# A router softmax on one core: hand-written synchronisation around all but the first loads, one filler matmul a trip, two rows cast early

## The chip, the cores and the metric

The kernel runs on one core of one Trainium2 chip. The metric is the device time of one execution in microseconds, the median of three runs. The profile is of one execution; its span runs from the first to the last profiled instruction and is a little shorter than the measured time.

## The reference

```python
# x: 16 x 512 x 1024 fp32, router_weights: 1024 x 8 fp32
logits = np.matmul(x, router_weights)
exp_logits = np.exp(logits - np.max(logits, axis=-1, keepdims=True))
return (exp_logits / np.sum(exp_logits, axis=-1, keepdims=True)).astype(np.float32)
```

There are 8192 tokens. Each has 1024 features, which are reduced to 8 logits, and a softmax runs over the 8. Nearly all of the traffic is the read of `x`, 33.6 MB.

## The kernel before

A token is named by a partition `p` (of P = 128) and a "row" `j` (of J = 64): row j is one tile of 128 tokens by 1024 features. Every row takes the same way. It is loaded and cast to bf16 in `x_all`; TensorE (PE) turns it in eight transposes of 128 x 128 (`loop_turn`, `turn`), five into the PSUM tile `ptv` and three into `pts`; VectorE copies the five to `xTv` and ScalarE the three to `xTs`; PE multiplies the eight chunks with the weights (`multiply`, eight matmuls with 8 columns each) into one place of the PSUM tile `lg`. After a group of eight rows VectorE and ScalarE do its softmax in five steps (`group` on VectorE, `power` on ScalarE), which are strewn between the copies.

All five engines are programmed by hand, with a semaphore for each dependence, inside one block of the framework, `tc.tile_critical()` (line 65), to which the framework adds an entry and an exit with a barrier of all engines (its instructions carry the lines 65 and 439 in the profile).

- **Loads.** SyncE (SP) issues rows 0 to 3 as fp32 into `x_f32`, in two transfers of two rows (line 130, semaphores `s_f`). ScalarE issues the weights (line 298) and casts the four rows to bf16 (line 304). GpSimd (POOL) issues all other rows with a cast on the way (line 150): twelve loads of four rows, three of two and five of one; row 63 comes in three pieces (line 163). Between the second and third of its loads GpSimd makes the identity and the filler's operand (lines 154 to 160).
- **Passing on.** SyncE waits for each cast and each landing and adds the number of rows to `s_xr` (lines 133 to 138), from which PE takes one for each row it turns (line 194). Later SyncE issues two stores of the result (lines 141 and 143) and waits for both (line 145).
- **The loop.** PE runs a hardware loop of 31 trips (line 263). A trip is: a filler matmul of 512 columns into a spare bank, whose result nobody reads; row 2t+1 turned; row 2t multiplied; a second filler; row 2t+2 turned; row 2t+1 multiplied. Instructions made by the helpers `again` have the line of what they were copied from, so in the loop all transposes have line 259 and all products and fillers line 246.
- **ScalarE's order.** Four casts, then one copy out of `pts` a row (line 319) and one exponential a group (line 309).
- **The tail.** After the loop the pieces of row 63 are turned, row 62 and row 63 are multiplied, and the last three rows get a softmax of their own (lines 376 to 413).

```python
        for k in range(LOADS[0]):
            if k % 2 == 0:
                act.wait_ge(s_f[k // 2], 16)
            act.copy(xa[:, k, :], x_f32[:, k, :]).then_inc(s_cast, 1)
```

Of the kernel before, what the change touches and what calls it, by code (L numbers as in the profile page):

```python
# [10 lines left out]
def kernel(  # L11
# [6 lines left out]
    nc = tc.nc  # L18
# [46 lines left out]
    with tc.tile_critical():  # L65
        X_AT = place[0]
        xa = sb("x_all", [P, J, D], bf16)
        x_f32 = sb("x_f32", [P, LOADS[0], D], fp32)
        identity = sb("identity", [P, P], bf16)
        ident = sb("ident", [P, P], fp32)  # L70
        w8 = sb("w8", [KO, P, N], fp32)
        w_bf = sb("w_bf", [P, KO, N], bf16)
        outv = sb("outv", [P, J, N], fp32)
        filler = sb("filler", [P, 512], bf16)
        xTv = [sb(f"xTv{i}", [P, VN, P], bf16) for i in range(2)]
        xTs = [sb(f"xTs{i}", [P, SN, P], bf16) for i in range(2)]
        xTz = [sb(f"xTz{i}", [P, n, P], bf16) for i, n in enumerate(PIECES)]
        mx = [sb(f"mx{i}", [P, G, 1], fp32) for i in range(2)]
        ex = [sb(f"ex{i}", [P, G, N], fp32) for i in range(2)]
        ev = [sb(f"ev{i}", [P, G, N], fp32) for i in range(2)]  # L80
        ssum = [sb(f"ssum{i}", [P, G, 1], fp32) for i in range(2)]
        inv = [sb(f"inv{i}", [P, G, 1], fp32) for i in range(2)]
        low = sb("low", [P, ALONE], fp32)
        ev3 = sb("ev3", [P, ALONE, N], fp32)
        sum3 = sb("sum3", [P, ALONE, 1], fp32)
        inv3 = sb("inv3", [P, ALONE, 1], fp32)


        LG_AT = 0x2000000
        lg = ps("lg", [P, 2, G, 64], fp32)  # L90
        ptv = [ps(f"ptv{i}", [P, 8, P], bf16) for i in range(2)]
        pts = [ps(f"pts{i}", [P, 8, P], bf16) for i in range(2)]
        spare = ps("spare", [P, 512], fp32)
        extra = ps("extra", [P, 8, 64], fp32)

        sem = tc.alloc_semaphore
        s_f = [sem(f"s_f{i}") for i in range(2)]
        s_w = sem("s_w")
        s_ld = [sem(f"s_ld{i}") for i in range(len(LOADS))]
        s_z = [sem(f"s_z{i}") for i in range(len(PIECES))]  # L100
        s_cast = sem("s_cast")
        s_m = sem("s_m")
        s_d = sem("s_d")
        s_id = sem("s_id")
        s_idb = sem("s_idb")
        s_fill = sem("s_fill")
        s_wt = sem("s_wt")
        s_wb = sem("s_wb")
        s_xr = sem("s_xr")
        s_tv = sem("s_tv")  # L110
        s_ts = sem("s_ts")
        s_cv = [sem(f"s_cv{i}") for i in range(2)]
        s_cs = [sem(f"s_cs{i}") for i in range(2)]
        s_zt = [sem(f"s_zt{i}") for i in range(len(PIECES))]
        s_zc = [sem(f"s_zc{i}") for i in range(len(PIECES))]
        s_p = sem("s_p")
        s_ex = sem("s_ex")
        s_ev = sem("s_ev")
        s_low = sem("s_low")
        s_e3 = sem("s_e3")  # L120
        s_out = sem("s_out")
        s_st = [sem(f"s_st{i}") for i in range(2)]

        first = [sum(LOADS[:i]) for i in range(len(LOADS))]
        cols = [sum(PIECES[:i]) for i in range(len(PIECES))]


        sp = nc.sync
        for i in range(2):
            sp.dma_start(  # L130
                out=x_f32[:, 2 * i:2 * i + 2, :], in_=x_rows[:, 2 * i:2 * i + 2, :]
            ).then_inc(s_f[i], 16)
        for k in range(LOADS[0]):
            sp.wait_ge(s_cast, k + 1).then_inc(s_xr, 1)
        for i in range(1, len(LOADS)):
            n = min(LOADS[i], LOOP_T + 1 - first[i])
            if n > 0:
                sp.wait_ge(s_ld[i], 16).then_inc(s_xr, n)
        sp.wait_ge(s_z[0], 16)
        sp.wait_ge(s_out, NG - 1)  # L140
        sp.dma_start(out=out_rows[:, 0:DONE, :], in_=outv[:, 0:DONE, :]).then_inc(s_st[0], 16)
        sp.wait_ge(s_out, NG + 1)
        sp.dma_start(out=out_rows[:, DONE:J, :], in_=outv[:, DONE:J, :]).then_inc(s_st[1], 16)
        for s in s_st:
            sp.wait_ge(s, 16)


        for i, r in enumerate(LOADS):
            if i:
                nc.gpsimd.dma_start(  # L150
                    out=xa[:, first[i]:first[i] + r, :], in_=x_rows[:, first[i]:first[i] + r, :]
                ).then_inc(s_ld[i], 16)
            if i == 2:
                nc.gpsimd.memset(ident, 0.0).then_inc(s_m, 1)
                nc.gpsimd.wait_ge(s_m, 1)
                nc.gpsimd.affine_select(  # L156
                    out=ident, in_=ident, compare_op=ALU.not_equal, fill=1.0, base=0,
                    pattern=[[-1, P]], channel_multiplier=1,
                ).then_inc(s_id, 1)
                nc.gpsimd.memset(filler, 0.5).then_inc(s_fill, 1)  # L160
        for i, n in enumerate(PIECES):
            c = slice(cols[i] * P, (cols[i] + n) * P)
            nc.gpsimd.dma_start(out=xa[:, J - 1, c], in_=x_rows[:, J - 1, c]).then_inc(s_z[i], 16)  # L163


        pe = nc.tensor
        r_x = [pe.alloc_register(f"rx{c}") for c in range(KO)]
        r_l = pe.alloc_register("rl")
        for c, r in enumerate(r_x):

            pe.reg_mov(r, X_AT + D * 2 + c * P * 2 + (P - 1) * 2)
        pe.reg_mov(r_l, LG_AT + 256 * SKIP)

        def at(ap, like, r):
            return mybir.RegisterAccessPattern(
                ap=ap, dtype=like.dtype, memsetref=like.tensor.name + "_set",
                regref=r.name, is_regloc_offset=False, reg_ap_offset=r.name,
                const_ap_offset=0, const_sub_tensor_id=0,
            )

        def again(like, **k):
            return pe.add_instruction(copy.replace(like, name=f"I-{nc.next_id()}", **k))

        def turn_ap(b, c):
            return (ptv if c < VN else pts)[b][:, c if c < VN else c - VN, :]

        def chunk(b, c):
            return xTv[b][:, c, :] if c < VN else xTs[b][:, c - VN, :]

        def loop_turn(b):  # L190

            for c in range(KO):
                if c == 0:
                    pe.wait_ge(s_xr, 1).then_inc(s_xr, -1)
                t = again(
                    turn_like,
                    ins=(turn_like.ins[0], at([[J * D, P], [1, P]], xa, r_x[c])),
                    outs=(pe.lower_ap(turn_ap(b, c), opt=False),),
                )
                if c == VN - 1:  # L200
                    t.then_inc(s_tv, 1)
                if c == KO - 1:
                    t.then_inc(s_ts, 1)
            for c in range(KO):
                pe.reg_add(r_x[c], r_x[c], D * 2)

        def turn(j):
            for c in range(KO):
                t = pe.transpose(turn_ap(j % 2, c), xa[:, j, c * P:(c + 1) * P], identity)
                if c == VN - 1:  # L210
                    t.then_inc(s_tv, 1)
                if c == KO - 1:
                    t.then_inc(s_ts, 1)
            return t

        def multiply(b, dst):

            for c in range(KO):
                if c == 0:
                    pe.wait_ge(s_cv[b], 1).then_inc(s_cv[b], -1)  # L220
                if c == VN:
                    pe.wait_ge(s_cs[b], 1).then_inc(s_cs[b], -1)  # L222
                if dst is None:
                    m = again(
                        mult_like,
                        ins=(
                            pe.lower_ap(w_bf[:, c, :], opt=False),
                            pe.lower_ap(chunk(b, c), opt=False, for_matmul_weights=True),
                        ),
                        outs=(at([[2 * G * 64, P], [1, N]], lg, r_l),),  # L230
                        start_tensor_calc=(c == 0),
                        stop_tensor_calc=(c == KO - 1),
                    )
                else:
                    m = pe.matmul(
                        dst, lhsT=chunk(b, c), rhs=w_bf[:, c, :],
                        start=(c == 0), stop=(c == KO - 1),
                    )
                if c == KO - 1:
                    m.then_inc(s_p, 1)  # L240
# [203 lines left out]
```

## Time and profile before

| | |
|---|---|
| time, median of 3 runs (lowest to highest) | 93.55 us (93.3 to 93.58) |
| span of the profiled execution | 91.8 us |
| PE busy on matmuls | 66.0 us, 72% |
| VectorE, ScalarE, GpSimd busy | 38.2, 38.4, 13.4 us |
| read from HBM, mean rate over the span | 33.59 MB, 369 GB/s |
| filler matmuls, count and mean | 63, 400 ns |

An entry such as `L342 DVE COPY xTv<-ptv` names the line, the engine, the operation and the tiles it writes and reads. PEld are PE's loads of the stationary operand, which run beside its matmuls. A name with a q (SPq) is the engine's queue: waits, semaphores and issues of transfers, which are not counted as busy. Matmuls overlap, so their durations do not add up; the distance between starts tells the pace. In the row of slices each digit is a fortieth of the span, 2.3 us, and 9 means nine tenths busy or more.

### The profile page before, as it was taken

How to read it: one execution, taken by the hardware profiler on the slowest of the kernel's cores; microseconds unless marked ns; L12 is line 12 of the kernel's file. 1: busy time of each engine (PE TensorE's matmuls, PEld its weight loads, DVE VectorE, ACT ScalarE, POOL GpSimd, SP SyncE). 2: the span in 40 equal slices, each digit the busy share in tenths (PEclk: the TensorE clock that was granted, in tenths of full speed). 3: DMA queues.
4: the chain of work that ended last, by engine and by line, in shares of the span. 5: the costliest groups of instructions: out<-in, count | busy, mean ns of one | idle time of the engine just before them, and what ended most of it. 6: DMA issues, size and time to landing. Idle time of an engine off the chain costs nothing.

```text
span 91.8 us, 3012 instructions
## 1 busy us (share of the span) xinstructions
PE 66.0 (72%) x1096; PEld 58.3 (63%) x1096; DVE 38.2 (42%) x113; ACT 38.4 (42%) x80; POOL 13.4 (15%) x30
## 2 busy tenths in 40 slices
PE   0519102998888888888888888888888888888300
PEld 0408001888877777888777777777777888777100
DVE  0202100245554555455445545554554455447500
ACT  3253038245444544454445444544444454447300
POOL 4899994000000000000000000000000000000000
PEclk9999999999999999999999999999999999999975
DMA  2999999999999999999999999999999999960000
GB/s 43 361 339 278 286 225 200 225 228 211 211 207 228 221 203 203 229 225 211 200 221 228 218 203 207 228 225 214 189 220 209 210 209 208 202 132 26 0 20 0
DMA packets 3906, 18.14 MB, mean 198 GB/s; under 512 B 568, under 2 KB 1080, under 8 KB 2112
## 3 DMA queue, kind: packets, MB, share of 16 engines
q0 software_dynamic: 3312, 15.73, 83.8%
q1 hardware_dynamic: 576, 2.36, 6.7%
q10 hardware_dynamic: 16, 0.03, 0.3%
q14 instruction: 2, 0.02, 0.0%
HBM read 33.59 MB, written 0.26 MB: 369 GB/s over the span
## 4 chain that ended last, share of the span: by engine, by line
PE 66%; issue 9%; DVE 1%; ACT 1%
PE spare L246 22%; PE ptv L259 19%; PE lg L246 12%; PE pts L259 12%; PE spare L290 1%; ACT xTz L329 1%; ACT xTs L319 0%; DVE low L378 0%; ACT ev L313 0%; DVE outv L369 0%; DVE inv L409 0%; DVE outv L411 0%; DVE sum L407 0%; DVE inv L365 0%
## 5 line engine op out<-in xcount | busy, mean ns | idle before, releaser
L342 DVE COPY xTv<-ptv 128x640 bf16<-128x640 bf16 x63 | 31.0, 491 | 43.5 <-PE ptv L259 40.5
L319 ACT COPY xTs<-pts 128x384 bf16<-128x384 bf16 x63 | 30.0, 478 | 37.0 <-PE pts L259 37.0
L246 PE MATMUL spare<-filler 128*128 128x512 bf16 x63 | 25.2, 400 | 7.9 <-issue 7.9
L259 PE MATMUL ptv<-identity,x_all 128*128 128x128 bf16 x311 | 28.8, 225 | 1.9 <-PEq L258 1.9
L259 PEld LDWEIGHTS ptv<-identity,x_all 128*128 (+1 forms) x311 | 23.2, 100 | 6.4 <-issue 3.4
L259 PE MATMUL pts<-identity,x_all 128*128 128x128 bf16 x186 | 21.3, 225 | 0.0
L246 PE MATMUL lg<-w_bf,xTs 128*128 128x8 bf16 x186 | 13.4, 166 | 6.1 <-PEq L222 6.1
L246 PE MATMUL lg<-w_bf,xTv 128*128 128x8 bf16 x310 | 16.9, 167 | 0.0
L246 PEld LDWEIGHTS lg<-w_bf,xTv 128*128 128x128 bf16 x310 | 14.7, 98 | 0.0
L259 PEld LDWEIGHTS pts<-identity,x_all 128*128 x186 | 13.6, 101 | 0.0
L246 PEld LDWEIGHTS lg<-w_bf,xTs 128*128 128x128 bf16 x186 | 9.1, 96 | 6.1 <-issue 6.1
L246 PEld LDWEIGHTS spare<-filler 128*128 128x128 bf16 x63 | 6.1, 97 | 10.5 <-issue 10.4
L150 POOL DMA_DIRECT2D x_all<-in_x_dram x20 | 10.7, 615 | 1.0 <-SPq L65 1.0
L304 ACT CAST x_all<-x_f 128x1024 bf16<-128x1024 f32 x4 | 4.0, 1042 | 8.2 <-DMA x_f<-in_x_dram 8.2
L253 PE MATMUL extra<-ident,w 8*128 8x8 f32 x8 | 1.0, 255 | 3.4 <-POOL ident L156 3.4
L253 PEld LDWEIGHTS extra<-ident,w 8*128 8x128 f32 x8 | 0.9, 198 | 3.4 <-POOL ident L156 3.4
L309 ACT ACTIVATE ev<-ex 128x64 f32<-128x64 f32 (+1 forms) x8 | 2.0, 254 | 0.3 <-DVE ex L354 0.3
L336 DVE CAST identity<-ident 128x128 bf16<-128x128 f32 x1 | 0.5, 518 | 3.4 <-POOL ident L156 3.4
L304 ACT ACT_TABLE_LOAD x1 | 1.3, 1283 | 1.5 <-SPq L65 1.5
L163 POOL DMA_DIRECT2D x_all<-in_x_dram x3 | 1.7, 704 | 0.0
L369 DVE TENSOR_TENSOR outv<-ev,inv 128x64 f32<-128x64 f32 (+1 forms) x8 | 1.7, 214 | 0.0
L354 DVE TENSOR_TENSOR ex<-lg,mx 128x64 f32<-128x64 f32 (+1 forms) x8 | 1.7, 213 | 0.0
(36 smaller groups left out, 14.8 us busy)
## 6 DMA issues: line engine op xcount, KB each, us to landing
x_all<-in_x_dram POOLq DMA_DIRECT2D x12, 1024.0 KB, 34.2
x_f<-in_x_dram SPq DMA_DIRECT2D x2, 1024.0 KB, 8.2
x_all<-in_x_dram POOLq DMA_DIRECT2D x3, 512.0 KB, 62.4
x_all<-in_x_dram POOLq DMA_DIRECT2D x5, 256.0 KB, 66.5
out_dram<-outv SPq DMA_DIRECT2D x1, 212.0 KB, 2.0
x_all<-in_x_dram POOLq DMA_DIRECT2D x1, 128.0 KB, 68.1
x_all<-in_x_dram POOLq DMA_DIRECT2D x2, 64.0 KB, 67.9
out_dram<-outv SPq DMA_DIRECT2D x1, 44.0 KB, 1.5
```

Source lines behind the costliest of these rows:

```text
L150: nc.gpsimd.dma_start(out=xa[:, first[i]:first[i] + r, :], in_=x_rows[:, first[i]:first[i] + r, :]).then_inc(s_ld[i], 16)
L163: nc.gpsimd.dma_start(out=xa[:, J - 1, c], in_=x_rows[:, J - 1, c]).then_inc(s_z[i], 16)
L246: return pe.matmul(spare, lhsT=filler[:, 0:P], rhs=filler, start=True, stop=True)
L253: t = pe.transpose(w_ps[:, n, :], w8[:, :, n], ident[0:KO, 0:KO])
L259: turn_like = pe.transpose(turn_ap(0, 0), xa[:, 0, 0:P], identity).ins
L290: m = pe.matmul(alone[2], lhsT=xTz[i][:, c, :], rhs=w_bf[:, cols[i] + c, :], start=(k == 0), stop=(k == KO - 1),)
L304: act.copy(xa[:, k, :], x_f32[:, k, :]).then_inc(s_cast, 1)
L309: act.activation(ev[g % 2][:, 0:n, :], ex[g % 2][:, 0:n, :], func=Exp).then_inc(s_ev, 1)
L319: act.copy(xTs[j % 2], pts[j % 2][:, 0:SN, :]).then_inc(s_cs[j % 2], 1)
L342: dve.tensor_copy(out=xTv[j % 2], in_=ptv[j % 2][:, 0:VN, :]).then_inc(s_cv[j % 2], 1)
L354: dve.tensor_tensor(out=ex[b][:, 0:n, :], in0=rows, in1=mx[b][:, 0:n, :].broadcast_to([P, n, N]), op=ALU.subtract,).then_inc(s_ex, 1)
L369: dve.tensor_tensor(out=outv[:, starts[g]:ends[g], :], in0=ev[b][:, 0:n, :], in1=inv[b][:, 0:n, :].broadcast_to([P, n, N]), op=ALU.mult,). ...
```

## The change

There are four edits.

1. The framework's part holds only the issue of the first three transfers (two of `x_f32`, the weights), in `tc.manual_schedule()`. It is closed right behind them with `tc.close()` and `tc.compile()`, which put its closing barrier and its clear of semaphores there. Everything else is written to the engines afterwards, and no instruction of the framework follows the wait for the last store. The purpose is to have no closing barrier at the end.
2. For that, the semaphores of the first transfers lie outside those that the framework clears, and are taken back by hand (`then_inc(s_f[i], -16)`, `then_inc(s_w, -16)`); GpSimd gets a drain of its own behind its loads.
3. The second filler of a trip goes: 32 filler matmuls remain of 63.
4. ScalarE casts rows 0 and 1, does the first two copies out of PSUM, and only then waits for and casts rows 2 and 3, so that it need not hold back the first rows' copies until the second load has landed.

The diff, without the lines in which only the indentation changed:

```diff
-    with tc.tile_critical():
...
-        s_f = [sem(f"s_f{i}") for i in range(2)]
-        s_w = sem("s_w")
+    s_f = [nc.alloc_semaphore(f"s_f{i}") for i in range(2)]
+    s_w = nc.alloc_semaphore("s_w")
...
-        sp = nc.sync
-        for i in range(2):
-            sp.dma_start(
+    with tc.manual_schedule():
+        early = [
+            nc.sync.dma_start(
                 out=x_f32[:, 2 * i:2 * i + 2, :], in_=x_rows[:, 2 * i:2 * i + 2, :]
             ).then_inc(s_f[i], 16)
+            for i in range(2)
+        ]
+        early.append(
+            nc.scalar.dma_start(
+                out=w8, in_=router_weights.rearrange("(ko ki) n -> ko ki n", ko=KO)
+            ).then_inc(s_w, 16)
+        )
+        for t in early:
+            tc.no_tile_sem_insts.add(t.ins.name)
+    tc.close()
+    tc.compile()
+
+    sp = nc.sync
...
         nc.gpsimd.dma_start(out=xa[:, J - 1, c], in_=x_rows[:, J - 1, c]).then_inc(s_z[i], 16)
+
+    nc.gpsimd.drain()
...
-        pe.wait_ge(s_w, 16)
+    pe.wait_ge(s_w, 16).then_inc(s_w, -16)
...
     with pe.Fori(0, TRIPS):
         fill()
         loop_turn(1)
         multiply(0, None)
-        fill()
         loop_turn(0)
         multiply(1, None)
...
-        act.dma_start(
-            out=w8, in_=router_weights.rearrange("(ko ki) n -> ko ki n", ko=KO)
-        ).then_inc(s_w, 16)
-        for k in range(LOADS[0]):
-            if k % 2 == 0:
-                act.wait_ge(s_f[k // 2], 16)
-            act.copy(xa[:, k, :], x_f32[:, k, :]).then_inc(s_cast, 1)
+    def cast(i):
+        act.wait_ge(s_f[i], 16).then_inc(s_f[i], -16)
+        for k in (2 * i, 2 * i + 1):
+            act.copy(xa[:, k, :], x_f32[:, k, :]).then_inc(s_cast, 1)
...
+    cast(0)
     for j in range(J - 2):
         act_copy(j)
+        if j == 1:
+            cast(1)
         if j - 1 in ends[:-1]:
             power(ends.index(j - 1))
```

## The prediction

> **What bounds the kernel now.** I read the page first: span 91.8 us of 93.55 us measured, so 1.75 us lie outside the profile. The sections on engine time and on slices say
>
> ```profile
> PE 66.0 (72%) x1096; PEld 58.3 (63%) x1096; DVE 38.2 (42%) x113; ACT 38.4 (42%) x80; POOL 13.4 (15%) x30
> ...
> DMA  2999999999999999999999999999999999960000
> ```
>
> PE is at eight tenths through the middle, and the transfers are at nine from slice 1 to 34 (2.3 to 80 us) and end before the program does. Two streams run side by side, and the question is which sets the end. The waits of the SyncE queue, which passes each landing on to PE, give the pace of the loads:
>
> ```profile
> SPq L138 <- DMA x_all<-in_x_dram: 65.0, 19, 5.3
> ```
>
> Taken in stretches of 5 us, nearly each wait for a load of four rows is 4.8 us, and with the instructions between the landings are 4.85 us apart: 1.21 us a row. The view of line 138 has its last instruction, which passes on row 62, the last row of the loop:
>
> ```profile
> L138 SPq EVENT_SEMAPHORE  x20: 17/17/17, 15.1 to 80.7; - x20
> ```
>
> Next the timeline of PE, one trip in the middle (start, duration):
>
> ```profile
> 50.99 0.39 PE L246 MATMUL spare<-filler 128*128 128x512 bf16 x1 [0.30 <-issue]
> 51.21 0.44 PE L259 MATMUL ptv<-identity,x_all 128*128 128x128 bf16 x5
> ...
> 51.88 0.38 PE L246 MATMUL spare<-filler 128*128 128x512 bf16 x1
> 52.10 0.44 PE L259 MATMUL ptv<-identity,x_all 128*128 128x128 bf16 x5
> ...
> 53.19 0.39 PE L246 MATMUL spare<-filler 128*128 128x512 bf16 x1 [0.30 <-issue]
> ```
>
> A trip is 2.20 us for two rows, 1.10 us a row, and PE waits for no load in it: the idle time is the loop's own 0.30 us. So PE is a little faster than the loads but late: it starts on row 1 in earnest at 15.7 us and chases. Has it caught up at the end? The tail of the timeline:
>
> ```profile
> 82.96 0.44 PE L259 MATMUL ptv<-identity,x_all 128*128 128x128 bf16 x5
> ...
> 84.84 0.27 PE L279 MATMUL ptv<-identity,x_all 128*128 128x128 bf16 x2
> ...
> 86.87 0.34 SPq L143 DMA_DIRECT2D out_dram<-outv  x1
> ```
>
> Row 62 is turned at 82.96 although it was there at 80.7: PE is still 2.3 us behind. From there to the last store's issue are 3.91 us. What follows is not work. The store's semaphore is seen at 88.4; then the framework closes (views of lines 65 and 439):
>
> ```profile
> L65 POOLq DRAIN  x1: 1934/1934/1934, 88.7 to 88.7; - x1
> ...
> L439 POOLq EVENT_SEMAPHORE_RANGE_CLEAR  x1: 374/374/374, 91.1 to 91.1; - x1
> ```
>
> A drain of GpSimd, a barrier, a clear and a barrier: 88.44 to 91.79, 3.35 us.
>
> [...] Four rows are 2.10 MB read in 4.85 us, 432 GB/s[...]. [...] The trace shows the change once: the five turns of a row take 0.74 us until 20.2 us and 0.44 after. [...]
>
> **The change, part by part.**
> (1) Closing barrier gone: no instruction stands after SyncE's wait for the last store. All 3.35 us from 88.44 on lie on the path. The drain now written by hand follows GpSimd's issues, which end at 14.9 us now: even 1.93 us of it lie beside the loop. Gain 3.35 us.
> (2) One filler a trip fewer. It holds PE from 51.88 to 52.10, 0.22 us; a trip becomes 1.98 us, 0.99 us a row. VectorE's and ScalarE's copies (0.49 and 0.48 us a row) do not bind: the copy of row 33 ends at 52.18, its product began at 52.54 and would begin at 52.32. Over 31 trips this is 6.8 us, but loads give two rows only every 2.42 us, so all PE can win is its lag. It gains (2.42 - 1.98) x 2 = 0.88 us per four rows; from a lag of about 5 us (rows 12 to 15 landed at 22.8, row 12 is turned at 28) it has caught up after six loads, near row 36. After that PE waits for loads. At the end: row 62 is passed on at 80.68; from such an event to PE's first turn took 0.15 to 0.2 us in the case of row 0 (cast done 6.73, PE 6.9). Turn at 80.87 instead of 82.96: gain 2.1 us. The 3.91 us behind it stay: turn, product of row 61, VectorE's maximum, ScalarE's two copies, last products, softmax of three rows. Its other inputs, the pieces of row 63, land by 81.3, 81.6 and 82.0 (packet records) and are needed 0.95, 1.2 and 1.9 us after the turn: 81.8, 82.1, 82.7. No wait.
> (3) The framework's part is short and closes early. Behind SyncE's two loads stands a barrier. SyncE issues perhaps 0.07 us earlier (a NOP goes), until 1.74; then drains, a clear and barriers of the kind that now take 90.67 to 91.74, 1.07 us. GpSimd then issues its first load at about 2.8 instead of 1.44. If a drain there takes 1.93 us more, it is 4.7; if the barrier overlaps the issues, 2. I take 2.8. What hides it: x_f32 alone fills the engines (410 GB/s between 4 and 5 us, before GpSimd's first packet at 5.3) and its 2.1 MB need until about 7.4. GpSimd's first packet moves to 6.7 (5.9 to 8.6), so the stream has a gap of 0 to 1.2 us; I take 0.1. Queued behind GpSimd are ident, filler and through them PE's first turns, all done by 6 us, before row 0 is cast. The two take-backs of 16 are one more semaphore instruction each (17 ns on ScalarE's queue, 51 on PE's, in the view of line 439), ahead of waits that are longer: 0.
> (4) ScalarE: rows 0 and 1 are cast, then copied out of PSUM, then rows 2 and 3. Today the first copy waits behind all four casts, until 14.9. The order of the built program also has the table load (1.28 us) behind the wait for the first load, so the first cast moves from 5.7 to about 7. PE's product of row 0 no longer waits from 9.4 to 15.5. All of this changes when PE starts, and the lag is gone by the end anyway: 0 us.
> Sum: 3.35 + 2.1 - 0.1 = 5.35, 93.55 - 5.35 = 88.2 us.
>
> **The rivals.**
> A, as summed: 88.2 us, 74 in 100.
> B, PE cools while it waits. With one filler it is busy 62% of the time: 32 turns of 56 ns, 32 products of 25 and two fillers of 215 are 3.0 us in 4.85. At the slow rate a half trip with filler takes 1.49 us (17.23 to 18.73), without about 1.11, four rows 5.2 us; that is more than 4.85, so a cold PE never waits[...]. The tail would lose about 0.3 us on each group of eight turns and some on products, 0.8 in all: 89.0 us, 13 in 100.
> C, the end of the profile isn't the end of the measurement: if the 3.35 us are replaced by a wait outside the span, 91.5. For it: 1.75 us are outside now. Against: nothing shows them to overlap the close. 5 in 100.
> D, the early barrier waits for the loads in flight: GpSimd issues at about 8.6 and its packets start at 12.5, while x_f32 ends at 7.4: 5.1 us of idle engines, 93.3 us. SyncE's drains are 7 ns, but none stands before an open transfer. 3 in 100.
> E, slower: PE stays at the slow rate for good. 31 trips of 1.49 + 1.11 = 2.60 from 15 us end at 95.6; the 3.1 us after the loop (83.8 to 86.87) and 0.8 more put the store at 99.5, its landing 1.55 later at 101.1: 102.8 us measured. For it: PE is slow from 6.9 to 20.2 today. Against: at that rate it is never idle. 5 in 100 with everything else that ends above 93.8.
>
> **How the numbers follow.** A with the early gap (0 to 1.2) and half a microsecond on the load's rate holds 87.3 to 89.4, B reaches 90; C and above are left out: 87.3 to 90.0. Faster by more than 0.3% is A, B and C with a part of D: 0.93; within it the rest of D: 0.02; slower E: 0.05.
>
> **What would show it.** Right: the span ends with the wait for the last store, about 86.4; PE's idle time before turns is put down to loads or to SyncE from about row 36; row 62 is turned within 0.3 us of its landing; store issue 3.9 us later; the first GpSimd load near 2.8 and the last landing still near 82. Wrong: turns of 0.74 us past 25 us (B, E), a first GpSimd load after 5 us (D), a span near 86 with a time above 90 (C).

## The result and the profile after

The changed kernel takes 89.04 us (median of 4 runs, 88.88 to 89.33), the kernel before 93.56 us beside it: a ratio of 0.951, 95% interval 0.944 to 0.957. It is 4.5 us faster. The forecast was 88.2 us with a range of 87.3 to 90.0.

The page of the changed kernel, engine time, granted clock and transfers by slices (each digit is a fortieth of 87.8 us):

```profile
span 87.8 us, 2937 instructions
...
PE 64.1 (73%) x1065; PEld 56.7 (65%) x1065; DVE 38.4 (44%) x113; ACT 38.4 (44%) x80; POOL 13.5 (15%) x30
...
PEclk9999999999999999999759999999958999999998
DMA  3999999999999999999999999999999999999200
```

The transfers fill the span as before. What is new stands in the row of the clock: twice, near the 20th and the 30th slice, PE was granted half speed (0.50, for 3.41 us each time). The same row of the kernel before:

```profile
PEclk9999999999999999999999999999999999999975
```

The lines of the framework and of the last wait, from the views by line:

```profile
L144 POOLq EVENT_SEMAPHORE  x4: 17/17/17, 1.9 to 2.7; - x4
...
L144 POOLq EVENT_SEMAPHORE_RANGE_CLEAR  x1: 330/330/330, 2.2 to 2.2; - x1
...
L160 SPq EVENT_SEMAPHORE  x1: 28/28/28, 87.8 to 87.8; - x1
```

The same wait in the kernel before:

```profile
L145 SPq EVENT_SEMAPHORE  x1: 17/17/17, 88.4 to 88.4; - x1
```

The barrier and the clear are over at 2.7 us, beside the first transfers, and the wait for the last store (line 160, at 87.76) is the end of the span. Before, 3.37 us followed it (88.42 to 91.79), now 0.03.

The loop, from PE's timeline (start, duration; row 57 is turned, that is transposed, at 77.16, row 58 at 77.96):

```profile
76.94 0.39 PE L263 MATMUL spare<-filler 128*128 128x512 bf16 x1 [0.35 <-issue]
77.16 0.44 PE L276 MATMUL ptv<-identity,x_all 128*128 128x128 bf16 x5
...
77.96 0.44 PE L276 MATMUL ptv<-identity,x_all 128*128 128x128 bf16 x5
...
79.10 0.39 PE L263 MATMUL spare<-filler 128*128 128x512 bf16 x1 [0.35 <-issue]
```

A trip is 2.16 us; it was 2.20. The second filler held PE for 0.22 us, and its removal shortens the trip by 0.04. The tail (row 62 turned, last piece turned, last store) and the line that passes row 62 on:

```profile
82.28 0.44 PE L276 MATMUL ptv<-identity,x_all 128*128 128x128 bf16 x5
...
84.16 0.27 PE L295 MATMUL ptv<-identity,x_all 128*128 128x128 bf16 x2
...
86.20 0.34 SPq L158 DMA_DIRECT2D out_dram<-outv  x1
```

```profile
L153 SPq EVENT_SEMAPHORE  x20: 17/17/17, 13.0 to 80.4; - x20
```

Row 62 is passed on at 80.4 and turned at 82.28, 1.9 us later. Before it was 2.3. From its turn to the last store's issue are 3.92 us, as before (3.91).

So the 4.5 us are, between the two profiled executions: 3.34 us behind the last store's wait; 0.67 us by which the tail comes earlier; and 0.46 us outside the span, which was 1.77 us in the profiled execution before and is 1.32 now.

### The profile page after: what moved, and what is told of

It reads as the page before. It is cut to its first block, busy times and chain, and to the rows that moved or that the text cites. A ratio compares the mean times of both kernels' runs of the same rounds, so it can differ in the third digit from the quotient of the medians.

```text
span 87.8 us, 2937 instructions
## 1 busy us (share of the span) xinstructions
PE 64.1 (73%) x1065; PEld 56.7 (65%) x1065; DVE 38.4 (44%) x113; ACT 38.4 (44%) x80; POOL 13.5 (15%) x30
## 3 DMA queue, kind: packets, MB, share of 16 engines
q0 software_dynamic: 3312, 15.73, 87.7%
## 5 line engine op out<-in xcount | busy, mean ns | idle before, releaser
L276 PE MATMUL ptv<-identity,x_all 128*128 128x128 bf16 x311 | 30.3, 233 | 6.2 <-PEq L211 4.8
L276 PEld LDWEIGHTS ptv<-identity,x_all 128*128 (+1 forms) x311 | 22.3, 103 | 10.4 <-issue 7.7
L276 PE MATMUL pts<-identity,x_all 128*128 128x128 bf16 x186 | 22.0, 230 | 0.0
L263 PE MATMUL spare<-filler 128*128 128x512 bf16 x32 | 13.7, 429 | 9.0 <-issue 8.9
L276 PEld LDWEIGHTS pts<-identity,x_all 128*128 x186 | 14.3, 105 | 0.0
L263 PEld LDWEIGHTS spare<-filler 128*128 128x128 bf16 x32 | 3.1, 98 | 11.6 <-issue 11.5
L318 ACT ACT_TABLE_LOAD x1 | 1.3, 1283 | 5.6 <-ACTq L316 5.6
L367 DVE TENSOR_REDUCE mx<-lg 128x8 f32<-128x64 f32 (+1 forms) x8 | 1.7, 214 | 0.0
```

The lines of the kernel that those rows point to most:

```text
L263: return pe.matmul(spare, lhsT=filler[:, 0:P], rhs=filler, start=True, stop=True)
L276: turn_like = pe.transpose(turn_ap(0, 0), xa[:, 0, 0:P], identity).ins
L367: dve.reduce_max(mx[b][:, 0:n, 0], rows, axis=X).then_inc(s_d, 1)
```

## The experiments

All are timed beside the kernel before, whose medians in these comparisons were 93.86 to 93.89 us. The changed kernel was timed beside a median of 93.56. So the ratios are what to compare, and a difference of medians between the changed kernel and another can be off by 0.3 us.

Two explanations of the lag at the end, the 1.9 us, stood against each other. The *backlog* theory: rows 48 to 51 land together, so at that moment PE has four rows before it, of which three count as late; from there to the landing of row 62 PE needs seven trips and the loads 13.6 us, and what PE needs more than that is the lag. The *clock* theory: the half-rate windows make it. On the trip there were two as well: the *array* binds it (then a filler costs its 0.22 us), or PE's own *instruction queue*, with its semaphore, register and branch instructions.

**Edits 1 and 2 alone**: the changed kernel with the second filler and the four casts as before.

```diff
         multiply(0, None)
+        fill()
         loop_turn(0)
...
     cast(0)
+    cast(1)
     for j in range(J - 2):
         act_copy(j)
-        if j == 1:
-            cast(1)
```

> Edits 1 and 2 alone: the framework's early close, with two fillers a trip and all four casts ahead of the first copies. Backlog theory: a trip stays 2.20 us and the start is earlier, so PE still meets the last four-row load with little lag; the span loses the 3.35 us behind the last store's wait and about 0.3 us at the start, the time the same and 0.4 us more that lie outside the span: 89.4 us. Rival, the gain is shared by all edits: well above that, 90.5 or more.

Measured: 89.55 us, ratio 0.958 (0.952 to 0.963). By the ratios the early close alone brings 4.2 of the changed kernel's 4.9%. The gain isn't shared by all edits. The early close also brings most of the earlier tail, with two fillers still in the trip. Row 62 in this kernel's PE timeline:

```profile
82.39 0.44 PE L276 MATMUL ptv<-identity,x_all 128*128 128x128 bf16 x5
```

That is 0.57 us earlier than the 82.96 of the kernel before, of the 0.68 that the changed kernel reaches.

**Edit 3 alone**: the kernel before without the second filler.

```diff
         multiply(0, None)
-        fill()
         loop_turn(0)
```

> Edit 3 alone: the kernel before with the second filler of a trip taken out. If the array's time binds the trip: 1.98 us, PE catches up and row 62 is turned 1.5 to 2 us earlier, 91.6 us. If PE's instruction queue binds it: trip 2.16 us, row 62 at most 0.5 us earlier, 93.1 us.

Measured: 93.13 us, ratio 0.993 (0.991 to 0.996): 0.7%, and a trip of 2.16 to 2.18 us. The array does not set the trip; that the instruction queue does is shown further down. The 0.7 and the 4.2 add up to the whole, but the sum is an accident, for at the tail the two do the same work. Here row 62 is turned at 82.09, 0.87 us earlier than before, since the shorter trips bring PE level with the loads at row 48 (it is turned 0.17 us after it lands); the early close alone has 0.57, and both together have 0.68.

**The second filler put back** into the changed kernel (the first hunk of edits 1 and 2 alone).

> The changed kernel with the second filler put back. Queue theory: trip 2.20 us instead of 2.16, over the eight trips after the last four-row load 0.3 us, time 89.3. Array theory: trip 2.4 us or the lag grows, time above 90. Clock theory (the half-rate windows at 42.8 and 63.3 us make the lag at the end): with two fillers PE stays at full rate and the time falls below 88.7.

Measured: 89.42 us, ratio 0.953 (0.949 to 0.957); trip 2.20 us. PE kept the full clock, 1.00 from 20 to 86 us. Here are the stretch in which the changed kernel lost it (the second) and the one ahead of it, in the profile of this kernel:

```profile
39.37:42.78 3.41, 2.42 (x45) 1.93 (x42) 1.57 (x4) 1.43 (x3) 0.00 (x0) 1.00 1.00 209
42.78:46.20 3.42, 2.69 (x50) 2.44 (x50) 1.54 (x5) 1.22 (x3) 0.00 (x0) 1.00 1.02 213
```

The columns are the window, its length, busy time and count of PE, PEld, VectorE, ScalarE and GpSimd, granted clock, share of the transfers, GB/s. The clock is 1.00, and the kernel is not faster: the medians differ by 0.38 us the other way, the ratios by 0.25%, within their intervals. Row 62 is turned at

```profile
82.32 0.44 PE L276 MATMUL ptv<-identity,x_all 128*128 128x128 bf16 x5
```

2.0 us after it landed. So the half-rate windows are not the main cause of the lag. They have a small share in it: in the changed kernel the second window ends at 66.68, and row 48 is turned 0.34 us after its landing instead of 0.17 here.

The spans of this kernel's seven executions are 87.7 to 87.9 us, those of the changed kernel's four 87.6 to 88.0. Inside the span, then, the second filler costs nothing that can be seen; what differs is the time outside the span, 1.60 to 1.65 us in six of the seven (2.64 in one) against 1.28 to 1.33.

**No filler in the loop.**

```diff
     with pe.Fori(0, TRIPS):
-        fill()
         loop_turn(1)
```

> The changed kernel with no filler in the loop. Queue theory: the trip falls by no more than 0.1 us, to about 2.08, since the first turn of a trip waits for its own instructions; array theory: by 0.22 us to 1.94. PE stands more and has more half-rate windows than the two of the changed kernel; if one of them falls on the tail, 89.5, else 88.6 to 89.0.

Measured: 89.18 us, ratio 0.950 (0.946 to 0.953), no different from the changed kernel. PE's timeline of this kernel, two first turns of a trip and the second turn between:

```profile
76.97 0.44 PE L276 MATMUL ptv<-identity,x_all 128*128 128x128 bf16 x5 [0.45 <-PEq L211]
...
77.89 0.44 PE L276 MATMUL ptv<-identity,x_all 128*128 128x128 bf16 x5
...
79.13 0.38 PE L276 MATMUL ptv<-identity,x_all 128*128 128x128 bf16 x4 [0.45 <-PEq L211]
```

The trip is still 2.16 us. Where the filler was, PE stands, and the profile names its sequencer (PEq) at line 211, the wait in front of a turn; the rows waited for had landed 2.3 us and more before, so it is not a load that PE waits for. My 0.1 us for the last filler was too much: the trip is no shorter without it. The mean clock of this profile is 0.887, by far the lowest of all, and the time is the same.

**The loop's body written twice**: half of the counter and branch instructions.

```diff
-    with pe.Fori(0, TRIPS):
+    with pe.Fori(0, TRIPS // 2):
         fill()
         loop_turn(1)
         multiply(0, None)
         loop_turn(0)
         multiply(1, None)
+        fill()
+        loop_turn(1)
+        multiply(0, None)
+        loop_turn(0)
+        multiply(1, None)
+    fill()
+    loop_turn(1)
+    multiply(0, None)
+    loop_turn(0)
+    multiply(1, None)
```

> The changed kernel with the loop's body written twice, 15 trips and one body behind the loop: the same matmuls, half of the counter and branch instructions. Queue theory: two bodies take about 3.95 us instead of 4.32, because the 0.35 us of idle time in front of a filler are the branch; the backlog of the last four-row load is then gone before row 62, which is turned about 1.3 us earlier: 87.7 us. If the array or the copies bind the trip: no change, 89.0.

Measured: 87.99 us, ratio 0.938 (0.935 to 0.942), 1.05 us under the changed kernel. The same matmuls: two bodies take 1.82 and 2.17 us, 3.99 instead of 4.32. PE's timeline:

```profile
49.02 0.39 PE L263 MATMUL spare<-filler 128*128 128x512 bf16 x1 [0.21 <-issue]
...
50.84 0.38 PE L263 MATMUL spare<-filler 128*128 128x512 bf16 x1
...
81.04 0.44 PE L276 MATMUL ptv<-identity,x_all 128*128 128x128 bf16 x5 [0.17 <-PEq L211]
```

The body without a branch behind it is 1.82 us long (49.02 to 50.84), and row 62 is turned at 81.04, 1.24 us earlier than in the changed kernel. The span falls with it, from 87.8 to 86.5 us. So neither the array nor the copies of VectorE and ScalarE bind the trip of 2.16 us: they do the same work in both bodies. The branch and the counter, with what they hold up, cost 0.34 us a trip. The branch alone has a median of 208 ns in the queue of the changed kernel:

```profile
L280 PEldq COMPARE_BRANCH  x31: 76/208/229, 13.0 to 83.1; - x31
```

What bounds the 1.82 us that remain is not shown.

**Smaller loads**: rows 36 to 57 two by two.

```diff
-    LOADS = [4] * 13 + [2, 2, 2] + [1] * 5
+    LOADS = [4] * 9 + [2] * 11 + [1] * 5
```

> The changed kernel with rows 36 to 57 in eleven loads of two rows instead of four of four and three of two. Backlog theory: the 1.9 us by which row 62 is turned after it landed are the rest of three rows that the last four-row load leaves waiting; with two-row loads it falls to about 0.5 us, time 87.7. Clock theory: the lag is made by half-rate windows, and more waits make more of them: 89 us or above.

Measured: 87.69 us, ratio 0.935 (0.931 to 0.939): 1.35 us under the changed kernel. PE's timeline has row 62 at

```profile
80.77 0.44 PE L276 MATMUL ptv<-identity,x_all 128*128 128x128 bf16 x5
```

0.34 us after it was passed on (80.43). No instruction of PE was touched; only the lumps in which rows arrive. This profile has a half-rate window too, from 48.5 to 51.9 us. The backlog theory holds for the changed kernel.

**Smaller loads in the kernel before**, the same line.

> The kernel before with rows 36 to 57 in loads of two rows, nothing else changed. Backlog theory: PE's lag of 2.6 us at row 36 falls by 0.12 us a row (1.22 less 1.10) and is gone before row 60; row 62 is turned 1.5 to 2 us earlier, 91.5 to 92.2 us. If only the changed kernel can make use of small loads (earlier start, one filler): 93.5.

Measured: 94.14 us, ratio 1.002 (1.000 to 1.004): no gain, the expectation failed. The trace tells why: from the fourth trip on every trip is 2.20 to 2.24 us. This PE never waits for a load, so no load can help it; its end is its start plus 31 trips. I had taken its lag at row 36 against a four-row load; against the two-row load it is 4.3 us (landed at 50.1, turned at 54.4), 2.3 at row 52, and 2.1 at row 62. The lag of the kernel before is thus that of a late start, not of its last four-row load. The changed kernel has been level with the loads since row 20: that row lands at 32.33 and, after PE has waited, is turned at 32.50.

```profile
32.50 0.44 PE L276 MATMUL ptv<-identity,x_all 128*128 128x128 bf16 x5 [0.25 <-PEq L211]
```

**Both**: smaller loads and the body twice.

> Two-row loads and the loop's body written twice together. Backlog theory: either alone brings row 62 to its landing, so both together bring no more than one: 87.7 us, within 0.25. If the two gains were of different kinds they would add: 86.6.

Measured: 87.76 us, ratio 0.934 (0.931 to 0.937): no better than the smaller loads alone. Both spend the same lag; row 62 is turned 0.16 us after it is passed on, and nothing is left to gain there.

**Edit 4 undone** in the changed kernel.

```diff
     cast(0)
+    cast(1)
     for j in range(J - 2):
         act_copy(j)
-        if j == 1:
-            cast(1)
```

> Edit 4 undone: all four casts ahead of the first copies. Backlog theory: PE starts later and is level with the loads somewhat later, still before row 40; row 62 is turned at the same time: 89.0 us, within 0.2. Rival, the early start matters to the end: 89.5 or more, as the kernel with two fillers and four casts.

Measured: 89.05 us, ratio 0.949 (0.945 to 0.953). Edit 4 brings nothing here. The view of `x_f` shows that its purpose is gone as well. Before, and in the changed kernel:

```profile
DMA to landing us min/median/max: 4.7/8.2/11.6
```

```profile
DMA to landing us min/median/max: 4.7/6.4/8.0
```

The second transfer of `x_f32` lands 8.0 us after its issue instead of 11.6 (at 9.2 us, not 13.0). GpSimd's packets start at 7.2 us instead of 5.3, so it has the transfer engines to itself for longer; that this is the reason is read from the times, no run isolates it. The casts of rows 2 and 3 are hardly held up any more: with all four in front, ScalarE waits 0.4 us for them.

**The drain at the end**: GpSimd's drain moved behind the last store's wait.

```diff
+    for s in s_st:
+        nc.gpsimd.wait_ge(s, 16)
     nc.gpsimd.drain()
```

> The changed kernel with GpSimd's hand-written drain moved behind the last store's wait, where the framework's exit had it: the price of the drain alone. If the drain takes 1.93 us whenever it first follows GpSimd's loads, the span grows by 2.0 us and the time to 91.0. If it took so long only inside the framework's exit: 89.1.

Measured: 91.42 us, ratio 0.973 (0.970 to 0.976), 2.4 us over the changed kernel. The view of its line:

```profile
L182 POOLq DRAIN  x1: 1932/1932/1932, 87.6 to 87.6; - x1
```

The drain is as long as in the framework's exit (1934 ns), 70 us after the last instruction GpSimd had to do. It alone is more than half of what the close cost. Between the profiled executions the difference is 2.26 us: 1.74 in the span, where the tail was 0.24 us earlier, and 0.52 outside it (1.84 us against 1.32). This profile has no half-rate window in the loop.

In the changed kernel, where the drain stands behind GpSimd's last issue, it looks different:

```profile
L180 POOLq DRAIN  x1: 68766/68766/68766, 13.9 to 13.9; - x1
```

It lasts until 82.67, 1.0 us after the last load has landed (81.69), and so is over 5.1 us before the span ends. It costs nothing there.

## Why the prediction held, and where its working was wrong

The forecast had the sign, the main term and the time within 0.84 us. The span it missed by more: 86.4 us forecast, 87.8 measured. That the time came closer is luck, since the time outside the span shrank by 0.46 us, which no term of the sum had. By its own steps:

**(1) The closing barrier.** Priced at 3.35 us, measured 3.34. That nothing takes its place is shown: SyncE's wait ends the span. The drain written by hand was taken to last 1.93 us; it lasted 68.8, beside the loop as forecast. Case C was wrong in its direction: the time outside the span did not grow.

**(2) The filler** is the step that failed, in the sentence "a trip becomes 1.98 us". The filler's time on the array was subtracted from a trip that the array doesn't set. The runs with two, one and no filler have trips of 2.20, 2.16 and 2.16 us, and the body without a branch takes 1.82: what binds the trip is PE's instruction queue, its branch above all (208 ns of the 0.34 us). The trace before had the sign in it: 0.30 us of idle time "issue" ahead of a filler, which the prediction took as a fixed addition to the trip and not as what bound it. With 2.16 us the gain of 2.1 us on row 62 shrinks:

| | loads of rows 48 to 51 to row 62 landed | seven trips, row 48 turned to row 62 turned | row 48 turned after it landed | row 62 turned after it landed |
|---|---|---|---|---|
| before | 13.64 us | 15.43 us | 0.51 us | 2.30 us |
| edits 1 and 2 alone | 13.63 us | 15.47 us | 0.17 us | 2.01 us |
| edit 3 alone | 13.64 us | 15.12 us | 0.17 us | 1.65 us |
| changed | 13.64 us | 15.20 us | 0.34 us | 1.90 us |
| changed, the drain at the end | 13.64 us | 15.12 us | 0.17 us | 1.65 us |
| body twice | 13.64 us | 14.15 us | 0.17 us | 0.68 us |
| with 1.98 us a trip, an estimate | 13.64 us | 13.86 us | 0.17 us | 0.39 us |

The columns come from landings (66.74 and 80.38 us in the changed kernel) and PE's timelines; the last column is the second of them less the first, plus the third. The last row takes the prediction's trip and the 0.17 us that a level PE needs. The row of the body twice is measured and shows that with a shorter trip the lag does go, so the trip was the mis-sized term. The lag also can't fall to nothing once PE is level with the loads, which the step left out: a four-row load hands PE three rows too many at once. The changed kernel and the one with the drain at the end have the same loop; the first has two half-rate windows, the second ending where row 48 lands, and 0.25 us more lag. Over whole executions even that isn't seen: of the changed kernel's four, the one that kept the full clock throughout was the slowest (89.33 us).

In these sums the 0.68 us by which row 62 is turned earlier are 0.28 from the stream of loads (below), 0.17 from a smaller lag at row 48, and 0.23 from the seven trips. Edits 1 and 2 alone have 0.57 of them.

**(3) The early barrier.** GpSimd's first load is issued at 3.31 us, not 2.8: the framework's part goes on to 2.75 and GpSimd takes 0.5 us more. The cost was put at 0.1 us and has the other sign: `x_f32` is issued 0.2 us earlier (0.74 for 0.95) and lasts until 9.2 us, so GpSimd's first packet at 7.2 finds the engines busy (410 to 434 GB/s from 3 to 7 us), and the last load lands 0.28 us earlier (81.69 for 81.97). That the pace of the loads would stay was an assumption; the stream took 81.0 us from its first issue to its last landing before, and 80.9 now.

**(4) The casts**, costed at nothing: shown for edit 4 (ratios 0.949 without it and 0.951 with it). But the step's remark that the start of PE does not matter passed over what the early close does to it. With `x_f32` landed at 9.2 us instead of 13.0, row 2 is turned at 12.1 us instead of 16.1, with or without edit 4 (12.3 without). These 4 us are why PE is level with the loads at row 20, earlier than the row 36 forecast; with two fillers it is level at row 24, and with edit 3 and the late start only at row 48. For the tail any of these is early enough.

**Rival B**, a PE at half rate in the loop, happened: two windows of 3.41 us at a granted clock of 0.50, 42.8 to 46.2 and 63.3 to 66.7. That waiting makes them was its supposition and is not shown. The loop lost little by them, at most the 0.25 us of lag above. That its 89.0 us lies next to the 89.04 measured is chance: its 0.8 us were to come from a slow tail, and the tail ran at the full clock (1.00 from 66.7 to 87.1 us). The result also lies within the 89.4 us that the range left to A, but that room was meant for a gap in the loads and for their rate, and the last load landed earlier than before. **Rivals D and E** didn't occur: SyncE's drain behind the open transfers took 0.13 us at most, and the turns took 0.44 us over most of the loop (0.65 to 0.74 only up to 15.5 us and in the two windows).

Of the signs it named for being right, the 3.9 us behind row 62 and a last landing near 82 came true. The end of the span, the first GpSimd load near 2.8 us and row 62 turned within 0.3 us of its landing did not.

What stays open is why the time outside the span is shorter. Over all executions it is 1.7 to 2.1 us with the framework's exit (2.5 in one), 1.8 to 1.9 with GpSimd's drain last, and 1.3 to 1.65 in the kernels that end with SyncE's wait, apart from three executions with 2.5 to 2.6. What ends last has a part in it, but not alone: among those that end with SyncE the two with two fillers have 1.6, those with the body twice 1.4, the others 1.3. No run takes it apart. Most of what the filler's removal brings in the changed kernel lies here.

## What to carry to other kernels

Taking out an instruction saves its time only where that time sets its engine's pace (here the filler's 0.22 us took 0.04 off the trip): compare the trip with one that lacks it, or look for "issue" and PEq idle time, before subtracting. Where the consumer nearly kept up with its loads, as PE did here, the last large load decided the end: it handed over four rows at once, and the trips behind it took longer than the loads (15.20 us against 13.64), so that row 62 still lagged by 1.90; smaller last loads brought 1.35 us, the second filler's removal 0.4, most of it outside the span. But this held only for a consumer that was level with its loads: the same smaller loads brought nothing to the kernel before (ratio 1.002). And what the framework put behind the last store was pure time here, 3.34 us; what it puts behind the first load's issue, until 2.75 us, was free, because the load in flight, `x_f32` until 9.2 us, covered it.

## What the runs showed of the hardware that was not expected

PE ran at half rate in two windows of 3.41 us, and its longest idle times near them were 1.40 us, up to 43.08, and 0.56 us, up to 62.01. The windows of the changed kernel, with the columns as above:

```profile
35.96:39.37 3.41, 2.51 (x50) 2.30 (x49) 1.38 (x5) 1.05 (x3) 0.00 (x0) 1.00 1.06 221
39.37:42.78 3.41, 1.96 (x39) 1.67 (x36) 1.44 (x4) 1.44 (x3) 0.00 (x0) 1.00 1.07 223
42.78:46.20 3.42, 3.12 (x38) 2.94 (x39) 1.21 (x3) 0.96 (x2) 0.00 (x0) 0.50 0.95 199
...
59.85:63.26 3.41, 2.16 (x44) 1.85 (x41) 1.40 (x3) 1.44 (x3) 0.00 (x0) 1.00 0.98 204
63.26:66.68 3.42, 3.42 (x39) 3.04 (x39) 1.34 (x4) 1.11 (x3) 0.00 (x0) 0.50 1.02 211
```

The two windows at half rate (clock 0.50) each follow one in which PE was busy for 1.96 and 2.16 us of 3.41; a window with 2.51 us was followed by full rate. In the window from 59.85 us no two matmul starts lie more than 0.72 us apart. But busy time alone does not tell the two cases apart: with edits 1 and 2 alone a window of 2.06 us, from 40.61 us, was followed by full rate. In the changed kernel each window at half rate, in which PE was busy for 3.12 and 3.42 of 3.42 us, was followed by the full clock; without any filler two of the three half-rate stretches in the loop lasted two windows (6.83 us). What decides between 2.06 and 2.16 us is not shown.

GpSimd's first packet came 3.88 us after the issue of its first load in both kernels (1.44 to 5.32 and 3.31 to 7.19 us), although `x_f32` had been issued 0.5 us ahead of it in the one and 2.6 us in the other. This speaks against a queue behind `x_f32` and for a delay of that first load itself. The table load of ScalarE is 1283 ns in both kernels, and nothing is seen between it and the first cast: in the changed kernel the load runs from 5.59 to 6.87 us and the cast starts at 6.88. And GpSimd's drain after its loads took 1.93 us in the two kernels that had it at the end, 5.8 and 6.7 us after the last load had landed; issued behind the open loads, it lasted until 1.0 us after the last landing.
